# A decoder layer's routing: scratch in PSUM, one-hots eight tokens at a time, and two weight splits on another engine

## The chip, the cores and the metric

The kernel runs on one core of a Trainium2 chip. Its time is the device time of one execution in microseconds; of several runs the median counts. A core has TensorE (matrix products, into PSUM), VectorE, ScalarE and GpSimd, which work side by side, each through its own instructions in order, and queues that issue DMA transfers (SP's above all). VectorE and ScalarE reach both SBUF and PSUM; in this kernel GpSimd's operands are all in SBUF. PSUM has eight banks of 512 float32 values per partition.

## The reference

Two layers of a decoder work on 512 tokens of 1024 features. A layer has a token mixer, cross-attention into 256 memory rows, and a retrieval over 128 x 128 experts, each followed by a layer norm of the scaled input plus the result. The change lies in the second norm and in the first part of the retrieval:

```python
def peer_ffn(x, wq, k1, k2, u, v):
    qry = (x @ wq).reshape(B, S, PEER_HEADS, PEER_QDIM)            # 8 heads of 256
    s1 = jnp.einsum('bshc,nc->bshn', qry[..., :PEER_HALF], k1)     # 128 keys
    s2 = jnp.einsum('bshc,nc->bshn', qry[..., PEER_HALF:], k2)
    v1, i1 = lax.top_k(s1, PEER_TOPK)                              # 16
    v2, i2 = lax.top_k(s2, PEER_TOPK)
    cand = (v1[..., :, None] + v2[..., None, :]).reshape(B, S, PEER_HEADS, 256)
    sc, ci = lax.top_k(cand, PEER_TOPK)
    e1 = jnp.take_along_axis(i1, ci // PEER_TOPK, axis=-1)
    e2 = jnp.take_along_axis(i2, ci % PEER_TOPK, axis=-1)
    expert = e1 * N_KEYS + e2
    gate = jax.nn.softmax(sc, axis=-1)
    ...
        act = jax.nn.gelu(jnp.einsum('td,ted->te', xb, u[eb]), approximate=False)
        coef = (gb * act).astype(x.dtype)
        return jnp.einsum('te,ted->td', coef, v[eb])
```

## The kernel before

**Split products.** Large products are made in three passes: an operand is split into a high part (a cast on ScalarE, L224) and a low part (source minus high part, a subtraction, L225), and L229 to L231 multiply high by high, high by low and low by high. The subtraction runs on VectorE, or on GpSimd where the caller says so. `Weights` holds 256 columns of a projection as two pieces of 128 x 1024; `wahead(nl, ns)` issues the loads (L163, on SP's queue) and the splits of the groups that come next, on the engine in `weng`. `weights(ahead)` calls it and hands out the next group.

**Order.** The program is a list of instructions that a scheduler puts into an order for each engine, mostly that of the list; an instruction that is ready may pass one that is not. `weave` interleaves two streams of work by their estimated costs. SBUF scratch is handed out by `Arena`, in pages of 128 floats; memory that was given back first is given out first, so an instruction can wait for the last reader of what lay there before. PSUM tiles all come from one pool of eight banks (`bank`).

**Second norm.** `out_proj_ln` makes the rows of four blocks of 128 tokens; each block gets its residual (L312), statistics (L313, L319) and norm (L323, L300 to L304, L326) on VectorE, and is transposed (L280) and split for the queries. After it `body` sets `weng` to GpSimd and calls `queries`.

**Queries and routing.** `proj(h)` multiplies head h's query columns (48 instructions of 512 columns), copies the queries out (L791, ScalarE), makes the scores (L799) and copies them (L800). `main` does this for heads 1 to 7, with two chunks of the experts' first layer after each (one after heads 6 and 7); a chunk (`u_chunk`) is 24 products of 384 columns, with a Gelu on ScalarE (L1187), and its weights are split on GpSimd. Woven into it, `route(h)` runs on VectorE alone: for both halves of the keys `top16` finds the 16 largest values and their positions for each of four blocks (L840 to L848), L872 packs positions into bytes, L876 to L879 make 80 candidate sums, `top16` runs on these, and L885 to L906 decode the positions: which byte of which word belongs to each (L885 to L892), a shift count for four words (L898), the shift itself (L901), the maximum over the words (L903), a shift down (L905) and the expert's number (L906). All its scratch is in SBUF (`plain`).

**Gates.** Four chunks follow, then `gate_rows` for three blocks of 128 tokens, woven with two chunks, then four more chunks. Per block it splits the expert numbers into their two keys (L919 to L922), transposes them (L925) and the gates (L929), and for every four tokens makes a one-hot of the first key (L941, VectorE), multiplies it by the gates (L942, GpSimd), makes a one-hot of the second key (L948 on VectorE, or L945 and L946 on ScalarE for two of eight groups), multiplies the two (L951, TensorE) and copies the result (L952, ScalarE). The one-hots lie in the middle of SBUF, seven pieces of eight pages, of which the block's scratch `w` takes one. From 32 tokens on, a result goes to memory (L955) and comes back four chunks at a time in the dense part, where TensorE multiplies with all 128 chunks.

Of the kernel before, what the change touches and what calls it, by code (L numbers as in the profile page):

```python
# [65 lines left out]
def weave(*streams):  # L66
    """interleave generators that yield their costs, each with its estimated total"""
    live = [[g, 0.0, t] for g, t in streams]
    while live:
        s = min(live, key=lambda s: s[1] / s[2])  # L70
        try:
            s[1] += next(s[0])
        except StopIteration:
            live.remove(s)


class Arena:
# [21 lines left out]
    def take(self, shape, where):  # L99
        """where: 0 the first piece only, 2 its end, 1 the other pieces if possible, None any"""  # L100
# [37 lines left out]
class Split:  # L138
    """feature-major activations [128, 8, n] as two float32r parts, four blocks to a piece"""
# [13 lines left out]
class Weights:  # L153
    """256 (or fewer) columns of a projection: [128, 8, cols], loaded, then split"""
# [26 lines left out]
class K:  # L181
# [13 lines left out]
    def middle(self, arena):  # L195
        """hands the middle of SBUF to one of the two arenas"""
# [57 lines left out]
    def fm_proj(self, w, blocks, xT, outs, halves=None):  # L254
        """out [features, tokens] = w[:, 128 i:128 i + 128]^T x for i of blocks, if asked for by halves of the tokens,
        the first or the second half first"""
# [13 lines left out]
    def t_split(self, src, xT, tb, blocks):  # L270
        """src(i): [128 t, 128 f], to feature block blocks[i], tokens of tb"""
# [16 lines left out]
    def row(self, name, l):  # L288
        """a parameter vector on all partitions"""
# [5 lines left out]
    def rstd(self, out, var, scale, eps, t, v):  # L295
        """out = (var * scale + eps) ** -0.5; t and v are for the steps between"""
# [12 lines left out]
    def residual(self, x, f, q, st):  # L309
        """one half of the rows of a block of tokens, and its statistics"""  # L310
# [4 lines left out]
    def layer_norm(self, y, st, g, b):  # L315
        """layer norm of the rows of one block of tokens, in place"""
# [11 lines left out]
    def out_proj_ln(self, l, yT, order, gname, bname, X):  # L328
        """X <- LN(ALPHA X + y @ w); returns the split transpose of the new rows"""
# [25 lines left out]
    def mixer(self, l, xT):  # L355
# [41 lines left out]
        def gates():  # L397
            """forget gates: cumulative log sigmoid on partitions 0..3"""
# [89 lines left out]
    def feat_rms(self, ys, gcol, yT, b0):  # L488
        """root mean square of 256 features on partitions, times the gain, to blocks b0, b0 + 1"""
# [94 lines left out]
    def stick(self, h, P, sp, ls, ys):  # L584
# [3 lines left out]
        for j in reversed(range(NT)):  # L588
# [3 lines left out]
            if j + 1 < NT:  # L592
                nc.tensor.matmul(tb[:, 128:n], self.ones, sp[j + 1], start=False, stop=True)
                if j:
                    # the sum of the blocks of keys from j on
                    nc.gpsimd.tensor_add(sp[j][:, 128:], sp[j][:, 128:], sp[j + 1])
# [13 lines left out]
    def rglru(self, xp, gate):  # L610
# [4 lines left out]
        # per feature: 8 softplus(-lam), and halves of the biases of the sigmoids  # L615
# [13 lines left out]
        for i in range(2):  # L629
# [5 lines left out]
            # u = x (1 + 0.044715 x^2) of the output gate's gelu  # L635
# [5 lines left out]
        for i in range(2):  # L641
# [3 lines left out]
            # sigmoid(z) = (1 + tanh(z / 2)) / 2  # L645
# [7 lines left out]
            # 1 - a^2 = tanh(w) (1 + a^2), a = exp(-w)  # L653
# [18 lines left out]
    def mem_kv(self, l, kv):  # L672
        """keys (feature-major) and values (rows) of the memory, by head"""
# [102 lines left out]
    def queries(self, l, xT, peer):  # L776
        """queries, scores and top experts of all tokens"""
# [5 lines left out]
        def proj(h):  # L783
            w = self.weights()
            q = []
            for b in ([0, 1],) if h == 0 else ([0], [1]):
                bks = [self.bank() for _ in b]
                emit(self.fm_proj(w, b, xT, bks, None if h else 0))
                for bk in bks:
                    q.append(self.al((S,)))  # L790
                    nc.scalar.copy(q[-1], bk)  # L791
            w.free()
# [10 lines left out]
        def main():  # L803
            """the rest of the queries, and chunks of the experts' first layer"""
# [19 lines left out]
    def softmax(self, v):  # L824
        """of the 16 scores of each head, the largest first: [t, head, 16]"""
# [10 lines left out]
    def top16(self, groups):  # L836
        """sorted 16 largest and their positions of each (values, largest, positions); spoils the values"""
# [12 lines left out]
    def route(self, h, sc, ga, ef):  # L850
        """top experts of one head for all tokens: their scores to ga, their numbers to ef"""
        nc = self.nc
        ta, tb, sh = self.al((896,)), self.al((NT, NC)), self.al((2 * NT, 4, TOPK))
        part = lambda o, *s: ta[:, o:o + int(np.prod(s))].rearrange(
            "p (t n) -> p t n" if len(s) == 2 else "p (t i n) -> p t i n", t=s[0],
            **({} if len(s) == 2 else dict(i=s[1])))
        v = part(0, NT, 2, TOPK)
        ix = part(128, NT, 2, TOPK).bitcast(U32)
        i8 = ta[:, 256:288].bitcast(U8)
        ti = part(288, NT, TOPK).bitcast(U32)  # L860
        tv = ga[:, :, h, :]
        q = part(416, NT, TOPK).bitcast(U32)
        m = part(480, NT, TOPK).bitcast(U32)
        d = part(544, NT, TOPK)
        r = part(608, NT, 2, TOPK)
        en = part(736, NT, 2, TOPK).bitcast(U32)
        for i in range(2):
            self.top16([(sc[:, t, i, :], v[:, t, i, :], ix[:, t, i, :]) for t in range(NT)])
            yield 4.3
        self.fr(sc)  # L870
        # the numbers as bytes, four to a word
        nc.vector.tensor_copy(i8, ta[:, 128:256].bitcast(U32))  # L872
        # candidates: (0, 0..15), (1..7, 0..7), (8..15, 0)
        v1, v2 = v[:, :, 0, :], v[:, :, 1, :]
# [8 lines left out]
        # position q + m, m < 8: (0, m) for q = 0, (0, 8 + m) for 8, (q / 8 - 1, m) for 16..64, (8 + m, 0) for 72;  # L883
        # all in units of an eighth
        nc.vector.tensor_scalar(q, ti, 120, None, op0=OP.bitwise_and)  # L885
        nc.vector.tensor_scalar(m, ti, 7, 3, op0=OP.bitwise_and, op1=OP.logical_shift_left)
        nc.vector.scalar_tensor_tensor(d, q, 72.0, m, op0=OP.is_equal, op1=OP.mult)
# [455 lines left out]
```

## Time and profile before

| what | value |
|---|---|
| median of 3 runs | 3571.64 us (3571.11 to 3574.22) |
| the profiled execution's span, first to last instruction | 3569.5 us |
| mean granted clock of TensorE | 0.984 |
| TensorE busy (products) | 3431.9 us, 96% |
| VectorE busy | 2599.8 us, 73% |
| ScalarE busy | 1433.2 us, 40% |
| GpSimd busy | 1149.4 us, 32% |
| HBM traffic | 206 GB/s over the span |

A row of the profile gives an engine's line in the kernel, the operation, what it writes and reads (`out<-in`, by the program's tiles: `plain`, `mid` and `parts` are SBUF, `bk` is a PSUM bank, `x` the activations), shapes, and a count. In a timeline the first numbers are start and duration, and the bracket is the engine's idle time before the instruction with what it waited for. Neighbouring instructions of one engine overlap by some 0.1 us. DVE is VectorE, ACT ScalarE, POOL GpSimd, PE TensorE and PEld its weight loads. PEclk is the share of TensorE's full clock that was granted.

### The profile page before, as it was taken

The page shows a single profiled execution, that of the slowest core. Times are in us where ns is not written, and L with a number is a line of the kernel's source. Part 1 is how long each engine was busy: PE and PEld are TensorE (multiplying, and loading weights), DVE is VectorE, ACT ScalarE, POOL GpSimd, SP SyncE. Part 2 cuts the span into 40 slices and gives each one's busy share as a digit, 9 for nine tenths or more (in the row PEclk, how much of TensorE's full clock was granted, in tenths as well). Part 3 has the DMA queues.
Part 4 walks back from the last instruction along what each step waited for, and adds up shares of the span by engine and source line. Part 5 has one row for each costly group of instructions (what it writes and reads, how often), then busy time and mean ns, then how long its engine had stood idle before and what let it go on. Part 6 is the DMA issues. An engine that isn't in the chain of part 4 may idle for free.

```text
span 3569.5 us, 50379 instructions
## 1 busy us (share of the span) xinstructions
PE 3431.9 (96%) x18546; PEld 3027.0 (85%) x18546; DVE 2599.8 (73%) x5122; ACT 1433.2 (40%) x2411; POOL 1149.4 (32%) x833
## 2 busy tenths in 40 slices
PE   9999989799999999999999999887999999999998
PEld 6678878788999999999876788777989999999987
DVE  4675489987777777777746754899777777777776
ACT  5653232573333333333345533325633333333332
POOL 0110043583334333433101000535733433334340
PEclk9999999999999999999999999998999999999999
DMA  4142221369888888888511322223698888888883
GB/s 169 59 131 71 85 83 61 118 247 334 303 302 292 295 303 294 294 300 284 200 51 59 124 77 79 83 66 130 258 332 300 298 300 288 308 295 294 296 293 117
DMA packets 278568, 738.17 MB, mean 207 GB/s; under 512 B 21424, under 2 KB 119984, under 8 KB 275248
## 3 DMA queue, kind: packets, MB, share of 16 engines
q1 hardware_dynamic: 204592, 466.47, 38.7%
q0 software_dynamic: 73728, 268.47, 20.3%
q8 instruction: 146, 2.39, 0.3%
q14 instruction: 102, 0.84, 0.1%
HBM read 682.43 MB, written 52.43 MB: 206 GB/s over the span
## 4 chain that ended last, share of the span: by engine, by line
PE 84%; DVE 13%; DMA 1%; ACT 1%; issue 1%; POOL 1%; DVEq 0%; SPq 0%; POOLq 0%; ACTq 0%
PE bk L229 24%; PE bk L231 24%; PE bk L230 24%; PE bk L951 5%; DVE plain L848 1%; DVE plain L844 1%; DVE plain L842 1%; PE bk L770 1%; DVE plain L840 1%; DVE plain L846 1%; PE bk L571 1%; PE bk L741 1%; DVE plain L901 1%; PE bk L527 1%; DVE x L326 1%
## 5 line engine op out<-in xcount | busy, mean ns | idle before, releaser
L231 PE MATMUL bk<-parts 128*128 128x512 f32 (+1 forms) x3746 | 1352.0, 361 | 0.3
L230 PE MATMUL bk<-parts 128*128 128x384 f32 (+2 forms) x3752 | 1334.9, 356 | 0.0
L229 PE MATMUL bk<-parts 128*128 128x384 f32 (+1 forms) x3554 | 1278.2, 360 | 2.3 <-ACT parts L224 2.3
L224 ACT CAST parts<-plain 128x1024 fp32r<-128x1024 f32 (+2 forms) x787 | 658.1, 866 | 1270.7 <-PE bk L230 1146.0
L225 DVE TENSOR_TENSOR parts<-plain,parts 128x384 fp32r<-128x384 f32 (+2 forms) x743 | 727.1, 983 | 513.5 <-ACT parts L224 484.9
L231 PEld LDWEIGHTS bk<-parts 128*128 128x128 f32 x3746 | 704.8, 188 | 68.8 <-issue 1.5
L230 PEld LDWEIGHTS bk<-parts 128*128 128x128 f32 x3752 | 707.3, 189 | 63.7
L229 PEld LDWEIGHTS bk<-parts 128*128 128x128 f32 x3554 | 669.8, 188 | 65.0 <-ACT parts L224 2.9
L976 POOL DMA_INDIRECT mid<-peer_u,plain x256 | 359.0, 1402 | 561.7 <-DVE plain L1011 430.4
L976 POOL DMA_INDIRECT mid<-peer_v,plain x256 | 364.5, 1424 | 544.5 <-DVE mid L999 443.6
L229 PE MATMUL bk<-parts,mid 128*128 128x512 f32 (+2 forms) x912 | 350.8, 387 | 11.3 <-ACT mid L224 7.9
L230 PE MATMUL bk<-parts,mid 128*128 128x512 f32 (+2 forms) x912 | 326.7, 359 | 5.1 <-DVE parts L225 5.1
L1011 DVE SCALAR_TENSOR_TENSOR plain<-mid,plain 128x1024 f32<-128x1024 f32 x256 | 327.7, 1280 | 1.5
L999 DVE SCALAR_TENSOR_TENSOR mid<-mid,x 128x1024 f32<-128x1024 f32 x256 | 309.2, 1219 | 0.0
L231 PE MATMUL bk<-parts,mid 128*128 128x512 f32 (+2 forms) x720 | 253.1, 353 | 0.0
L224 ACT CAST mid<-plain 128x1024 fp32r<-128x1024 f32 x163 | 168.7, 1037 | 201.3 <-PE bk L231 102.1
L229 PE MATMUL bk<-mid,parts 128*128 128x256 f32 (+1 forms) x798 | 237.0, 297 | 0.0
L231 PE MATMUL bk<-mid,parts 128*128 128x256 f32 (+1 forms) x798 | 229.0, 287 | 0.0
L229 PEld LDWEIGHTS bk<-parts,mid 128*128 128x128 f32 (+1 forms) x912 | 172.5, 190 | 57.2 <-issue 16.7
L951 PE MATMUL bk<-mid 128*128 128x128 f32 x1536 | 198.9, 292 | 17.1 <-POOL mid L942 16.4
L951 PEld LDWEIGHTS bk<-mid 128*128 128x128 f32 x1536 | 190.8, 198 | 25.0 <-POOL mid L942 21.5
L225 POOL TENSOR_TENSOR mid<-plain,mid 128x1024 fp32r<-128x1024 f32 x24 | 58.1, 2430 | 469.6 <-ACT mid L224 437.7
(229 smaller groups left out, 3940.9 us busy)
## 6 DMA issues: line engine op xcount, KB each, us to landing
plain<-peer_uT SPq DMA_DIRECT2D x256, 512.0 KB, 5.1
plain<-peer_v SPq DMA_DIRECT2D x256, 512.0 KB, 4.1
gates<-plain SPq DMA_DIRECT2D x24, 2048.0 KB, 6.9
plain<-gates SPq DMA_DIRECT2D x64, 768.0 KB, 8.0
plain<-w_in SPq DMA_DIRECT2D x44, 512.0 KB, 5.1
plain<-xa_wkv SPq DMA_DIRECT2D x32, 512.0 KB, 4.2
plain<-peer_wq SPq DMA_DIRECT2D x32, 512.0 KB, 4.1
plain<-w_out SPq DMA_DIRECT2D x16, 512.0 KB, 4.4
```

Of the source, the lines that this page charges most:

```text
L224: nc.scalar.copy(hi, src)
L225: return (eng or nc.vector).tensor_sub(lo, src, hi.bitcast(F32))
L229: nc.tensor.matmul(out, lt[0], rt[0], start=first, stop=False)
L230: nc.tensor.matmul(out, lt[0], rt[1], start=False, stop=False)
L231: nc.tensor.matmul(out, lt[1], rt[0], start=False, stop=last)
L326: nc.vector.scalar_tensor_tensor(y[:, h], y[:, h], rs, b[:, h], op0=OP.mult, op1=OP.add)
L527: nc.tensor.matmul(sb[:, :n], P["fq"][r][po, i * 128:n], P["fk"][r][po, :n], start=True, stop=True)
L571: nc.tensor.matmul(zb[:, :n], P["sk"][r][po, q0:q0 + 128], P["sq"][r][po, q0:], start=True, stop=True)
L951: nc.tensor.matmul(bk[:, k, :], o2[:, k, :], o1[:, k, :], start=True, stop=True)
L976: nc.gpsimd.indirect_dma_start(out=t, out_offset=None, in_=self.a[n], in_offset=bass.IndirectOffsetOnAxis(ap=ei[:, s:s + 1], axis=0))
L999: nc.vector.scalar_tensor_tensor(u, u, 1.0, x, op0=OP.mult, op1=OP.mult, accum_out=act[:, s:s + 1])
L1011: nc.vector.scalar_tensor_tensor(acc, v, act[:, s:s + 1], acc, op0=OP.mult, op1=OP.add)
```

## The change

The scratch of `route` moves to two PSUM banks, `ps` and `pi`, such that each decode instruction has at most one operand in SBUF; the shift down becomes two instructions. `gate_rows` keeps its integer steps in a bank, and works on eight tokens at a time; ScalarE makes the second one-hot of every third group of eight. The first two query weight groups are split on VectorE: `weng` is set to GpSimd inside `proj(0)`, after its products, and the second group's split is issued there too. Comments are also taken out, without effect.

```diff
 def proj(h):
-    w = self.weights()
+    w = self.weights() if h else self.weights(0)
...
             nc.scalar.copy(q[-1], bk)
+    if h == 0:
+        self.wahead(2, 1)
+        self.weng = nc.gpsimd
     w.free()
...
 def route(self, h, sc, ga, ef):
-    ta, tb, sh = self.al((896,)), self.al((NT, NC)), self.al((2 * NT, 4, TOPK))
+    ta, tb, sh = self.al((512,)), self.al((NT, NC)), self.al((2 * NT, 4, TOPK))
+    ps, pi = self.bank(), self.bank((128, 2 * NT, 4, TOPK))
...
-    v = part(0, NT, 2, TOPK)
-    ix = part(128, NT, 2, TOPK).bitcast(U32)
...
+    v1 = part(ps, 0, NT, TOPK)
+    ix = part(ps, 64, NT, 2, TOPK).bitcast(U32)
+    ti = part(ps, 192, NT, TOPK).bitcast(U32)
+    m = part(ps, 256, NT, TOPK).bitcast(U32)
+    r = part(ps, 320, NT, 2, TOPK)
+    e1 = part(ps, 448, NT, TOPK).bitcast(U32)
+    v2 = part(ta, 0, NT, TOPK)
+    i8 = ta[:, 64:96].bitcast(U8)
+    q = part(ta, 128, NT, TOPK).bitcast(U32)
+    d = part(ta, 192, NT, TOPK)
+    e2 = part(ta, 256, NT, TOPK).bitcast(U32)
...
-    si, su = sh.bitcast(I32), sh.bitcast(U32)
+    si, su = pi.bitcast(I32), sh.bitcast(U32)
...
-    nc.vector.tensor_tensor(su, words[:, :, :, None].to_broadcast(shape), su, op=OP.logical_shift_left)
+    nc.vector.tensor_tensor(su, words[:, :, :, None].to_broadcast(shape), pi.bitcast(U32),
+                            op=OP.logical_shift_left)
+    en = part(ps, 320, NT, 2, TOPK).bitcast(U32)
...
-    nc.vector.tensor_scalar(en, en, 24, None, op0=OP.logical_shift_right)
-    nc.vector.scalar_tensor_tensor(ef[:, :, h, :], en[:, :, 0, :], float(NK), en[:, :, 1, :],
-                                   op0=OP.mult, op1=OP.add)
+    nc.vector.tensor_scalar(e1, en[:, :, 0, :], 24, None, op0=OP.logical_shift_right)
+    nc.vector.tensor_scalar(e2, en[:, :, 1, :], 24, None, op0=OP.logical_shift_right)
+    nc.vector.scalar_tensor_tensor(ef[:, :, h, :], e1, float(NK), e2, op0=OP.mult, op1=OP.add)
...
 def gate_rows(self, tb, ga, ef, dram, stages):
+    pe = self.bank((128, 4, 128)).bitcast(I32)
...
-    sh = [128, 4, NK]
+    GB = 8
+    sh = [128, GB, NK]
...
-        for q in range(0, GT, 4):
+        for q in range(0, GT, GB):
...
-            if q % 12 == 8:
-                for k in range(4):
+            if t // GB % 3 == 2:
+                for k in range(GB):
...
-            bk = self.bank((128, 4, NK))
-            for k in range(4):
-                nc.tensor.matmul(bk[:, k, :], o2[:, k, :], o1[:, k, :], start=True, stop=True)
-            nc.scalar.copy(stage[:, :, q:q + 4], bk.rearrange("p t e -> p e t"))
+            for b in range(0, GB, 4):
+                bk = self.bank((128, 4, NK))
+                for k in range(4):
+                    nc.tensor.matmul(bk[:, k, :], o2[:, b + k, :], o1[:, b + k, :], start=True, stop=True)
+                nc.scalar.copy(stage[:, :, q + b:q + b + 4], bk.rearrange("p t e -> p e t"))
...
 def body(self, out):
...
-        self.weng = nc.gpsimd
         self.queries(l, xT, peer)
```

## Rows read from the trace of the kernel before

**Rows 1.** Busy time by stretch: start:end, length, engines (instructions), clock, DMA share, GB/s.
```profile
424.00:484.00 60.00, 49.56 (x380) 47.31 (x379) 47.55 (x64) 20.27 (x31) 20.97 (x9) 0.91 0.28 91
484.00:680.00 196.00, 171.15 (x887) 154.46 (x885) 181.33 (x924) 61.77 (x94) 70.22 (x31) 0.92 0.20 62
680.00:793.00 113.00, 102.86 (x785) 98.26 (x786) 101.24 (x167) 91.13 (x212) 100.68 (x100) 0.97 0.56 226
815.00:1770.00 955.00, 954.86 (x4777) 862.13 (x4778) 709.60 (x906) 344.13 (x488) 355.08 (x249) 1.00 0.84 293
```

**Rows 2.** TensorE's waits from 424 to 815 us: total, times, longest.
```profile
PE bk L925 <- DVE mid L922: 18.2, 1, 18.2
```

**Rows 3.** Timeline of VectorE in the second norm: start, duration, instruction.
```profile
427.22 1.23 DVE L225 TENSOR_TENSOR mid<-plain,mid 128x1024 fp32r<-128x1024 f32 x1 [1.15 <-ACT mid L224]
...
439.33 0.15 DVE L301 TENSOR_TENSOR ln_r<-ln_t 128x1 f32<-128x1 f32 x1
...
440.09 1.42 DVE L326 SCALAR_TENSOR_TENSOR x<-x,ln_r,plain 128x512 f32<-128x512 f32 x2
...
451.73 2.24 DVE L301 TENSOR_TENSOR ln_r<-ln_t 128x1 f32<-128x1 f32 x1
...
458.64 5.55 DVE L326 SCALAR_TENSOR_TENSOR x<-x,ln_r,plain 128x512 f32<-128x512 f32 x2
```

**Rows 4.** Timeline of GpSimd in the second norm.
```profile
451.16 5.13 POOL L225 TENSOR_TENSOR mid<-plain,mid 128x1024 fp32r<-128x1024 f32 x2 [191.69 <-ACT mid L224]
...
458.54 2.34 POOL L225 TENSOR_TENSOR mid<-plain,mid 128x1024 fp32r<-128x1024 f32 x1
```

**Rows 5.** Groups of VectorE's instructions, 484 to 672 us: busy us, mean ns, idle before.
```profile
L840 DVE MAX8 plain<-plain 128x8 f32<-128x128 f32 x64 | 14.8, 279 | 15.7 <-ACT plain L800 8.4 <-PE bk L799 7.2
L901 DVE TENSOR_TENSOR plain<-plain 128x512 uint32<-128x512 uint32 x8 | 13.9, 1736 | 0.2
...
L898 DVE TENSOR_TENSOR plain<-lanes,plain 128x512 int32<-128x512 f32 x8 | 9.5, 1193 | 0.3
...
L891 DVE TENSOR_TENSOR plain<-plain 128x64 f32<-128x64 uint32 x8 | 3.9, 492 | 0.2
```

**Rows 6.** Timeline of VectorE in the last head's route.
```profile
656.42 0.07 DVE L848 MATCH_VALUE_LOAD plain<-plain 128x8 f32 x1
...
663.49 0.23 DVE L891 TENSOR_TENSOR plain<-plain 128x64 f32<-128x64 uint32 x1
...
664.06 0.69 DVE L898 TENSOR_TENSOR plain<-lanes,plain 128x512 int32<-128x512 f32 x1
```

**Rows 7.** Timeline of TensorE in the routing.
```profile
484.88 0.49 PE L799 MATMUL bk<-plain 128*128 128x128 f32 x2
...
585.25 1.22 PE L799 MATMUL bk<-plain 128*128 128x128 f32 x4 [3.93 <-ACT plain L791]
...
632.68 0.39 PE L799 MATMUL bk<-plain 128*128 128x128 f32 x2
...
653.22 0.34 PE L231 MATMUL bk<-parts 128*128 128x384 f32 x1
```

**Rows 8.** Busy time of a stretch at half clock, columns as in rows 1.
```profile
583.30:596.90 13.60, 8.99 (x32) 8.48 (x33) 13.57 (x89) 4.23 (x6) 4.72 (x2) 0.50 0.24 78
```

**Rows 9.** Groups of instructions, 680 to 794 us, columns as in rows 5.
```profile
L951 PE MATMUL bk<-mid 128*128 128x128 f32 x752 | 97.4, 291 | 8.8 <-POOL mid L942 8.4
L942 POOL TENSOR_TENSOR mid<-mid,mid 128x512 f32<-128x512 f32 x94 | 94.6, 1040 | 9.5 <-DVE mid L941 8.7 <-DMA gates<-plain 0.2
...
L941 DVE TENSOR_TENSOR mid<-bk,iota 128x512 f32<-128x512 f32 x91 | 60.2, 682 | 5.5 <-ACT mid L930 4.5 <-PE bk L951 0.9
...
L946 ACT ACTIVATE mid<-mid 128x512 f32<-128x512 f32 x22 | 13.9, 631 | 0.5
```

**Rows 10.** Timeline of ScalarE in the gates.
```profile
674.10 1.57 ACT L945 ACTIVATE mid<-iota,mid 128x128 f32<-128x128 f32 x5
...
727.10 2.03 ACT L952 COPY plain<-bk 128x512 f32<-128x512 f32 x4
```

More of the change, by code (lines that the diff above doesn't have):

```diff
@@ L852, in route, with part @@
         nc = self.nc
-        ta, tb, sh = self.al((896,)), self.al((NT, NC)), self.al((2 * NT, 4, TOPK))
-        part = lambda o, *s: ta[:, o:o + int(np.prod(s))].rearrange(
-            "p (t n) -> p t n" if len(s) == 2 else "p (t i n) -> p t i n", t=s[0],
-            **({} if len(s) == 2 else dict(i=s[1])))
-        v = part(0, NT, 2, TOPK)
-        ix = part(128, NT, 2, TOPK).bitcast(U32)
-        i8 = ta[:, 256:288].bitcast(U8)
-        ti = part(288, NT, TOPK).bitcast(U32)
-        tv = ga[:, :, h, :]
[L862 to L868, printed above, removed]
+        ta, tb, sh = self.al((512,)), self.al((NT, NC)), self.al((2 * NT, 4, TOPK))
+        ps, pi = self.bank(), self.bank((128, 2 * NT, 4, TOPK))
+        def part(t, o, *s):
+            return t[:, o:o + int(np.prod(s))].rearrange(
+                "p (t n) -> p t n" if len(s) == 2 else "p (t i n) -> p t i n", t=s[0],
+                **({} if len(s) == 2 else dict(i=s[1])))
+        v1 = part(ps, 0, NT, TOPK)
[9 more added lines that the diff above has]
+        e2 = part(ta, 256, NT, TOPK).bitcast(U32)
+        tv = ga[:, :, h, :]
+        for i, v in enumerate((v1, v2)):
+            self.top16([(sc[:, t, i, :], v[:, t, :], ix[:, t, i, :]) for t in range(NT)])
             yield 4.3
         self.fr(sc)
-        nc.vector.tensor_copy(i8, ta[:, 128:256].bitcast(U32))
-        v1, v2 = v[:, :, 0, :], v[:, :, 1, :]
+        nc.vector.tensor_copy(i8, ps[:, 64:192].bitcast(U32))
         s1 = [128, NT, 7, 8]
@@ L886, in route @@
         nc.vector.tensor_scalar(m, ti, 7, 3, op0=OP.bitwise_and, op1=OP.logical_shift_left)
+        nc.vector.tensor_scalar(r[:, :, 0, :], q, 8.0, 0.0, op0=OP.subtract, op1=OP.max)
+        nc.vector.tensor_scalar(r[:, :, 1, :], q, 8.0, 64.0, op0=OP.is_equal, op1=OP.mult)
         nc.vector.scalar_tensor_tensor(d, q, 72.0, m, op0=OP.is_equal, op1=OP.mult)
-        nc.vector.tensor_scalar(r[:, :, 0, :], q, 8.0, 0.0, op0=OP.subtract, op1=OP.max)
         nc.vector.tensor_add(r[:, :, 0, :], r[:, :, 0, :], d)
-        nc.vector.tensor_scalar(r[:, :, 1, :], q, 8.0, 64.0, op0=OP.is_equal, op1=OP.mult)
         nc.vector.tensor_sub(d, m, d)
@@ L914, in gate_rows @@
         w = self.al((1024,), F32, 1)
-        ei = w[:, 896:1024].bitcast(I32)
-        i12 = w[:, 0:256].rearrange("p (a b) -> p a b", a=2).bitcast(I32)
         f12 = w[:, 256:512].rearrange("p (a b) -> p a b", a=2)
         st = w[:, 512:896].rearrange("p (a b) -> p a b", a=3)
-        nc.vector.tensor_copy(ei, ef[:, tb].rearrange("p h k -> p (h k)"))
-        nc.vector.tensor_scalar(i12[:, 0], ei, 7, None, op0=OP.logical_shift_right)
-        nc.vector.tensor_scalar(i12[:, 1], ei, 127, None, op0=OP.bitwise_and)
-        nc.vector.tensor_copy(f12, i12)
+        pe = self.bank((128, 4, 128)).bitcast(I32)
+        nc.vector.tensor_copy(pe[:, 0], ef[:, tb].rearrange("p h k -> p (h k)"))
+        nc.vector.tensor_scalar(pe[:, 1], pe[:, 0], 7, None, op0=OP.logical_shift_right)
+        nc.vector.tensor_scalar(pe[:, 2], pe[:, 0], 127, None, op0=OP.bitwise_and)
+        nc.vector.tensor_copy(f12, pe[:, 1:3])
         pt = self.bank((128, 3, 128))
@@ L931, in gate_rows @@
         yield 2
-        sh = [128, 4, NK]
+        GB = 8
+        sh = [128, GB, NK]
         io = self.iota[:, None, :].to_broadcast(sh)
-        col = lambda i, t: (st if i == 2 else pt)[:, i, t:t + 4, None].to_broadcast(sh)
+        col = lambda i, t: (st if i == 2 else pt)[:, i, t:t + GB, None].to_broadcast(sh)
         for g in range(128 // GT):
             stage = stages[:, g % 2]
-            for q in range(0, GT, 4):
+            for q in range(0, GT, GB):
                 t = g * GT + q
-                o1, o2 = (self.al((4, NK), F32, 1) for _ in range(2))
+                o1, o2 = (self.al((GB, NK), F32, 1) for _ in range(2))
                 nc.vector.tensor_tensor(o1, col(0, t), io, op=OP.is_equal)
                 nc.gpsimd.tensor_mul(o1, o1, col(2, t))
-                if q % 12 == 8:
-                    for k in range(4):
+                if t // GB % 3 == 2:
+                    for k in range(GB):
                         nc.scalar.activation(o2[:, k], self.iota, AF.Abs, scale=-1.0, bias=st[:, 1, t + k:t + k + 1])
@@ L948, in gate_rows @@
                     nc.vector.tensor_tensor(o2, col(1, t), io, op=OP.is_equal)
-                bk = self.bank((128, 4, NK))
-                for k in range(4):
-                    nc.tensor.matmul(bk[:, k, :], o2[:, k, :], o1[:, k, :], start=True, stop=True)
-                nc.scalar.copy(stage[:, :, q:q + 4], bk.rearrange("p t e -> p e t"))
+                for b in range(0, GB, 4):
[3 more added lines that the diff above has]
+                    nc.scalar.copy(stage[:, :, q + b:q + b + 4], bk.rearrange("p t e -> p e t"))
                 self.fr(o1, o2)
-                yield 1.3
+                yield 2.6
             nc.sync.dma_start(dram[:, tb * (128 // GT) + g], stage)
```

## The prediction

> **What bounds the kernel now.** I read the busy time by stretch first [rows 1]. [...] The time to be had lies between 424 and 793 us, and in the same stretches of the second layer, which look alike. There TensorE is idle for 10.4 us in the second norm (424 to 484), 24.9 us in the routing (484 to 680) and 10.1 us in the gates (680 to 793), and the mean clock is 0.91, 0.92 and 0.97.
>
> The waits of TensorE say who is late: its longest is 18.2 us at the end of the routing, for VectorE's L922 [rows 2]. So the routing ends with VectorE (busy 181.3 of 196 us [rows 1]); the gates run on TensorE (102.9 of 113 us) with GpSimd (100.7) and VectorE (101.2) close behind.
>
> Then the instructions. In the second norm a clean second half of the layer norm (two of L326) takes 1.42 us; while GpSimd splits weights, L301 takes 2.24 instead of 0.15 us and the two of L326 take 5.55 us [rows 3]; GpSimd's splits stand in exactly these microseconds [rows 4]. In the routing L901 has a mean of 1.74 us, L898 1.19, L891 0.49 [rows 5], where an undisturbed one takes 0.69 (L898; L901 has the same 512 elements) and 0.23 us [rows 6]. MAX8, which also reads SBUF, has its clean 0.28 us in all 64 cases [rows 5]. What is stretched is the decode steps, by a GpSimd split that runs at that moment.
>
> **The change, part by part; one layer.**
>
> *Norm.* The splits of the first two query weight groups (four subtractions of 128x1024) go from GpSimd to VectorE. VectorE loses the stretching: in the third block of tokens 2.1, 2.1, 1.9 and 4.1 us for L301, L302, L304 and L326, in the fourth 2.1, 1.7 and 1.5, together 15.5 us (the first and the last of the third block are shown [rows 3]). It gains 4 x 1.23 = 4.9 us [rows 3]. One GpSimd split stays, the experts' first, which preload gives to GpSimd by name, and so perhaps 2 us of stretching. ScalarE's casts stay the same in number. The second group's split, and the load of the third group on SP's queue, are issued after head 0's products: both are needed a head later, and ScalarE and SP idle there. A new wait: head 0's first product waits for VectorE's split, which stands behind the third block's norm; behind it TensorE holds that block's transposes. Net VectorE -8 to -10 us. TensorE's idle 10.4 us and about 3 us of low clock bound the gain at 13; if the new wait costs what a norm of a block costs (some 6 us from residual to transposes, of which half is hidden), 6 are left. I take **-10 us** (6 to 13).
>
> *Routing.* After the change every decode step has at most one operand in SBUF. The stretching summed over eleven decode groups (mean less clean, times 8: 8.5 for L901, 4.0 for L898, and 1.3 to 2.2 for each of the other nine, as L891's 8 x 0.26 = 2.1) is 30 us [rows 5, 6]. Without it VectorE has 181.3 - 30 = 151 us of work in the stretch, of which about 10 are softmax and one-hots: 18 us for each of 8 heads. One more instruction per head (the two shifts) costs 0.1. But TensorE then feeds VectorE: from 484.88 to 653.56 us it works 168.7 us [rows 7], of which 6.6 are two gaps near 585 (one of 3.93 is shown; ScalarE's copy waited there for memory that a late decode step held), and in the stretch at half clock that follows, 9.0 us busy were worth 4.5 [rows 8]. That is 157.6 us without both. The last head's scores come at 633 now [rows 7], hence at 622 then; a copy of 1 us, 18 us of route, 4 us of softmax and of the gates' first steps, and 1.5 us of the head before not yet done: 646.5 against 671.7 now, 25 us less. The 18.2 us wait shrinks to about 4.
>
> What PSUM costs VectorE is only half shown. L941 with an operand in PSUM takes 0.68 us for 512 elements [rows 9], L898 with both in SBUF 0.69 [rows 6]: no difference. No row has a MAX8, an index or an integer step that reads or writes PSUM. Above I bound it by one MATCH_VALUE_LOAD (0.07 us, [rows 6]) for each of the 27 instructions of a head that read PSUM: 1.9 us a head. As heads come every 21 us and a route takes 18, that shows only in the last two heads: 0 to 4 us. I take 1, near the row. Routing: **-24 us**; ends -27 (nothing for PSUM, no head late) and -17 (the gaps near 585 stay). [...]
>
> *Gates.* Per four tokens TensorE needs 8 of 752 instructions that fill 97.4 us, 1.04 us, and GpSimd one product, 94.6 us for 94, 1.01 us [rows 9]: level. With eight tokens the elements stay, and instructions halve on VectorE and GpSimd. I expect nothing back, since TensorE needs its 1.04 anyway. What is lost: (a) a block's first unit goes through VectorE and GpSimd before TensorE may start, 0.68 + 1.04 us now, about 1.25 + 2.0 then: +1.5 us at each of two boundaries between blocks, +3. (b) The two one-hots of a unit now fill two pieces of eight pages; six of the middle's seven pieces are left beside the block's scratch, so three units are in flight instead of six half as big. ScalarE builds five of 16 units a block: 8 x 0.31 for L945 (five in 1.57 us) and about 0.95 for a L946 twice as wide as one of 0.63, 3.4 us, and has 4 copies of 0.51 (four in 2.03 us) beside [rows 9, 10], all in the 4 us that TensorE needs for the two units before: 5.4 against 4.0, so up to 1.4 us lost at four units of three blocks, 17 us; nothing, if the copies give way. I take +2: four copies in one piece show that copies do give way to L945 now. (c) GpSimd's 1024-element product: twice 1.01, or the 2.34 us of a split, a product's width with another operation [rows 4]: 48 x 0.32 = 15 us more. I take twice 1.01; L942 is the same operation on the same kinds of operands. Gates: **+5 us** (0 to 20). The integer steps in a PSUM bank instead of SBUF save 1 to 3 us of VectorE off the path: nothing.
>
> Sum: -10 - 24 + 5 = -29 us a layer, -58 in all. The profiled execution's span of 3569.5 becomes 3511.5; the median of the runs is 2.1 us above that span, so 3571.6 becomes **3514 us**.
>
> **The rivals.**
> - *The units of eight starve TensorE through ScalarE*: (b) at its full 17. For it: ScalarE is at 91.1 of 113 us already [rows 1] and gets 25% more one-hots. Against: copies can wait, with banks free. -10 - 24 + 20 = -14 a layer: 3544.
> - *GpSimd's wide product costs what a split costs*, GpSimd becomes the bound of the gates: -10 - 24 + 18 = -16: 3540. Against: twice L942 is below it.
> - *All goes well*: no loss in the gates, 12 in the norm, 27 in the routing: -39, 3494.
> - *The change doesn't free the decode*: L872 and other steps with a single SBUF operand are held too, and each new step still has one. Then 3 us in the routing, 6 in the norm, 5 lost: 3564. Against: MAX8 has one SBUF operand and is never held, nor is L941 (0.68 in all cases, beside a GpSimd busy for 100.7 of 113 us).
> - *Slower: banks.* A route now holds two of eight PSUM banks for all its 18 us; a head's products, scores and two chunks ask for six. If banks are given out so that one request must wait for a route to end, TensorE can't run ahead: a head then takes 11 (products) + 2 + 1 + 18 = 32 us instead of 21, last scores at 709, the routing's end 59 us later: +54 a layer, about 3680. It decides from the seventh request within one route on.
>
> **How the numbers follow.** Forecast 0.44 (3500 to 3530), ScalarE's units 0.17, GpSimd's product 0.13, all well 0.15, decode not freed 0.05, banks 0.06. The range goes from the good case with its last bounds to just beyond the two gates cases: 3485 to 3556. This kernel's measurement tells about 0.2% (7 us) from no change. Faster: the first four, 0.89; same: 0.05; slower: 0.06.
>
> **What would show it.** Right: L901 and L898 near 0.69 us in all 16 cases; L301, L302 at 0.15 in the second norm; TensorE's wait for L922 under 6 us; no half clock in the routing. Wrong: L951 waiting for ScalarE's L946 or for a L942 of more than 2.0 us; TensorE's products waiting for a bank that VectorE's route releases; MAX8 or FIND_INDEX8 above 0.35 us. A half clock in the gates would add to any of the losses.

## The result, and the profile after

The changed kernel is slower. Its median is 3597.72 us (3591.16 to 3598.77) against 3571.38 for the kernel before: a ratio of 1.0068, 95% interval 1.0053 to 1.0082. The forecast was 3514 with a range to 3556. The profiled execution's span is 3589.5 us, 20.0 above that of before.

Both layers lost alike (9.4 and 10.5 us). The table cuts the first layer of several kernels at four events of TensorE's and VectorE's timelines: the first product with the keys (head 0's scores), the first transpose of the gates (L925 before, L935 after), the end of the last matmul of the gates (L951, L963), and the end of the layer's last residual. The other kernels are the experiments below.

| us | scores start | routing, to the transposes | gates | rest of the layer | layer ends |
|---|---|---|---|---|---|
| before | 483.2 | 188.5 | 121.0 | 992.0 | 1784.7 |
| after | 479.6 | 193.3 | 127.0 | 994.2 | 1794.1 |
| route_only | 485.3 | 195.2 | 121.1 | 991.0 | 1792.6 |
| gates_only | 483.0 | 188.9 | 128.7 | 994.3 | 1794.9 |
| norm_only | 478.3 | 188.4 | 120.6 | 991.7 | 1779.0 |
| wide_scratch | 478.6 | 192.5 | 130.1 | 992.6 | 1793.8 |
| top16_in_sbuf | 484.9 | 178.4 | 128.8 | 993.2 | 1785.3 |
| two_banks | 480.4 | 177.7 | 129.3 | 993.5 | 1780.9 |
| norm_and_decode | 479.5 | 179.9 | 122.6 | 994.1 | 1776.1 |
| norm_chunks_too | 474.9 | 187.6 | 120.8 | 992.0 | 1775.3 |
| three_units | 483.4 | 187.7 | 131.9 | 992.8 | 1795.8 |
| six_units | 482.0 | 186.8 | 123.0 | 996.7 | 1788.5 |
| norm_u_decode | 473.0 | 179.8 | 122.3 | 991.6 | 1766.7 |

The first column is the least sure: top16_in_sbuf, two_banks and after share one norm and lie 5 us apart. These 5 us stand ahead of the norm. From the norm's first residual (L312) to the first scores, all kernels with the old norm take 69.3 or 69.4 us, all with the norm of the change 65.8 or 65.9 (norm_chunks_too 60.9, norm_u_decode 59.4), in the second layer of before and after too (69.3 and 65.8). So of after's 9.4 us, the norm gave some 3.5 back, the routing took 4.8, the gates 6.0 and the rest of the layer 2.2.

Busy time of after by stretch, columns as in rows 1, whose stretches these answer to:

```profile
424.00:480.00 56.00, 48.77 (x378) 46.75 (x376) 43.66 (x68) 19.88 (x31) 12.07 (x5) 0.91 0.31 97
480.00:680.00 200.00, 168.41 (x885) 151.81 (x885) 175.02 (x927) 61.45 (x92) 69.45 (x30) 0.94 0.20 64
680.00:800.00 120.00, 98.34 (x791) 95.27 (x790) 91.82 (x85) 98.58 (x229) 94.90 (x52) 0.96 0.51 207
```

VectorE's 181.3 us in the routing [rows 1] were to become some 151; they are 175.0. In the gates every engine is now idle for over 20 of 120 us: a chain of waits bounds them, not one engine's work. TensorE's waits in after, 424 to 830 us (total, times, longest):

```profile
PE bk L935 <- DVE mid L932: 22.6, 1, 22.6
PE bk L963 <- POOL mid L953: 10.9, 4, 3.7
PE bk L963 <- ACT mid L957: 9.3, 11, 1.1
PE bk L280 <- DVE x L326: 6.2, 3, 4.1
```

The first answers to rows 2: 22.6 us where 18.2 stood and 4 was forecast. The next two are the gates' matmuls waiting for GpSimd's products and for ScalarE's one-hots. The aim of the change itself was reached. VectorE's groups of after, 480 to 680 us (busy us, mean ns, idle before):

```profile
L907 DVE TENSOR_TENSOR bk<-lanes,bk 128x512 int32<-128x512 f32 x8 | 5.6, 695 | 0.4
L910 DVE TENSOR_TENSOR plain<-plain,bk 128x512 uint32<-128x512 uint32 x8 | 5.4, 680 | 0.1
...
L901 DVE TENSOR_TENSOR bk<-bk,plain 128x64 f32<-128x64 f32 x8 | 1.9, 232 | 0.3
...
L900 DVE TENSOR_TENSOR plain<-bk,plain 128x64 f32<-128x64 uint32 x8 | 1.8, 224 | 0.3
```

L910 and L907 are the L901 and L898 of rows 5, which had means of 1736 and 1193 ns; they now have their clean length while GpSimd splits as much as ever (69 of 200 us). So the question is what ate the gain.

### The profile page after: what moved, and what is told of

It reads as the page before. It is cut to its first block, busy times and chain, and to the rows that moved or that the text cites. A ratio compares the mean times of both kernels' runs of the same rounds, so it can differ in the third digit from the quotient of the medians.

```text
span 3589.5 us, 49948 instructions
## 1 busy us (share of the span) xinstructions
PE 3421.7 (95%) x18546; PEld 3017.5 (84%) x18546; DVE 2559.0 (71%) x4972; ACT 1446.9 (40%) x2441; POOL 1118.4 (31%) x729
## 5 line engine op out<-in xcount | busy, mean ns | idle before, releaser
L225 POOL TENSOR_TENSOR parts<-plain,parts 128x1024 fp32r<-128x1024 f32 x44 | 109.5, 2497 | 579.5 <-ACT parts L224 542.1
L963 PE MATMUL bk<-mid,mid 128*128 128x128 f32 x1536 | 188.7, 285 | 40.0 <-POOL mid L953 21.6
L963 PEld LDWEIGHTS bk<-mid,mid 128*128 128x128 f32 x1536 | 183.3, 199 | 45.3 <-POOL mid L953 27.8
```

The source lines that it names most:

```text
L225: return (eng or nc.vector).tensor_sub(lo, src, hi.bitcast(F32))
L963: nc.tensor.matmul(bk[:, k, :], o2[:, b + k, :], o1[:, b + k, :], start=True, stop=True)
```

## The experiments

**One part at a time.** Three kernels, each the kernel before with one function of the change. Ratios here and below are against runs of the kernel before that stand beside each group (medians 3572.9 to 3575.9 us).

```diff
 route_only: before, with the changed route()
 gates_only: before, with the changed gate_rows()
 norm_only: before, with
-    w = self.weights()
+    w = self.weights() if h else self.weights(0)
...
+    if h == 0: self.wahead(2, 1); self.weng = nc.gpsimd
...
-    self.weng = nc.gpsimd
```

> The kernel before with the change's routing alone (scratch in PSUM); norm and gates as before. Theory: two things cancel the freed decode. The decode steps lose their 33 us of held time a layer, the instructions of top16 that write a PSUM bank wait for each other and gain 24 us, and the first MAX8 waits for head 1's scores because the smaller scratch lies where head 1's query was: it starts about 10 us later, at 496 instead of 486.5 us. TensorE's wait for the gates' first step stays near 18 to 24 us; the time is 3565 to 3580 us. Rival, that the routing is the gain that was forecast and only the gates lose: first MAX8 near 487, that wait under 6 us, 3520 to 3535 us.

> The kernel before with the change's gates alone (eight tokens at a time, integer steps in a bank). Theory: ScalarE's share of the one-hots, every third unit, is late by 0.8 to 1.1 us at each of some 12 units a layer, and a block's first unit takes 1.4 us longer: +6 to +8 us a layer, 3583 to 3588 us. Rival, that the gates lose only in the company of the other parts: within 3 us of the kernel before, 3568 to 3575.

> The kernel before with the change's norm alone (the first two weight groups split on VectorE). Theory: GpSimd still does the experts' first split and the third group's in the norm and still holds up two steps of the last blocks; the first scores come 2 to 4 us earlier, 3563 to 3568 us. Rival, the full removal as forecast: first scores 10 us earlier, 3548 to 3555.

route_only: 3586.43 us, 1.0033 (1.0024 to 1.0043). gates_only: 3596.75 us, 1.0066 (1.0044 to 1.0089). norm_only: 3565.68 us, 0.9975 (0.9962 to 0.9989). The norm helps a little, as expected; the routing's scratch in PSUM, which the forecast counted on, is a loss by itself, 6 us above the upper end of its expectation; the gates are the largest loss, 9 us above theirs.

**The routing: a late start, or dearer sorting?** VectorE's timeline shows two new things in after. The routing starts late (the first MAX8 before, then in after):

```profile
486.52 0.49 DVE L840 MAX8 plain<-plain 128x8 f32<-128x128 f32 x2 [8.36 <-ACT plain L800]
```

```profile
492.93 0.29 DVE L843 MAX8 plain<-plain 128x8 f32<-128x128 f32 x1 [18.34 <-PE bk L802]
```

Scores begin 3.6 us earlier than before and MAX8 6.4 us later. It writes the second list's values into the 512-float scratch, which lies where head 1's query lay, and so it waits until head 1's scores (L802) have read that. And the index searches stand further apart. VectorE in the kernel before, then in after, near 520 us (start, duration, instruction):

```profile
520.61 0.29 DVE L842 FIND_INDEX8 plain<-plain 128x8 uint32<-128x128 f32 x1
520.81 0.07 DVE L842 MATCH_VALUE_LOAD plain<-plain 128x8 f32 x1
520.87 0.29 DVE L842 FIND_INDEX8 plain<-plain 128x8 uint32<-128x128 f32 x1
521.07 0.07 DVE L842 MATCH_VALUE_LOAD plain<-plain 128x8 f32 x1
521.12 0.29 DVE L842 FIND_INDEX8 plain<-plain 128x8 uint32<-128x128 f32 x1
```

```profile
520.10 0.29 DVE L851 FIND_INDEX8 bk<-bk,plain 128x8 uint32<-128x128 f32 x1
520.43 0.10 DVE L851 MATCH_VALUE_LOAD bk<-bk,plain 128x8 f32 x1
520.51 0.29 DVE L851 FIND_INDEX8 bk<-bk,plain 128x8 uint32<-128x128 f32 x1
520.84 0.10 DVE L851 MATCH_VALUE_LOAD bk<-bk,plain 128x8 f32 x1
520.92 0.29 DVE L851 FIND_INDEX8 bk<-bk,plain 128x8 uint32<-128x128 f32 x1
```

The durations are equal (0.29). But before, the next instruction starts 0.20 us after a search has started, while that one still runs, and the next search 0.26 us after the last; in after these are 0.33 and 0.41 us, and the search is over before anything starts. A sum of durations can't show that; the starts do. From start to start, less the waits for scores, the instructions of `top16` take 105 us a layer before and 128 in after (129 in wide_scratch, below); the rest of `route`, mostly the decode, takes 69.4 before and 44.1 after.

Two kernels part the causes. wide_scratch takes the late start away, top16_in_sbuf the writes of `top16` into PSUM as well.

```diff
 wide_scratch: after, with
-    ta, tb, sh = self.al((512,)), ...
+    ta, tb, sh = self.al((896,)), ...
 top16_in_sbuf: wide_scratch, with
-    v1 = part(ps, 0, NT, TOPK)
-    ix = part(ps, 64, NT, 2, TOPK).bitcast(U32)
-    ti = part(ps, 192, NT, TOPK).bitcast(U32)
+    v1 = part(ta, 0, NT, TOPK)
+    ix = part(ta, 128, NT, 2, TOPK).bitcast(U32)
+    ti = part(ta, 256, NT, TOPK).bitcast(U32)
...
```

> The changed kernel with the routing's SBUF scratch at its old size of 896 floats (more than it uses), which moves it off the memory of head 1's query. Theory: the first MAX8 no longer waits for head 1's scores and starts near 483 instead of 492.9 us, the routing's end comes 6 to 10 us a layer earlier, 3578 to 3586 us. Rival, that the late start comes from the PSUM banks: no change, 3595 to 3599.

> The run with the wide scratch, and in it all that top16 writes (both lists, their positions, the positions of the candidates) in SBUF; the decode's scratch stays in PSUM. Theory: top16 costs its old 105 us a layer instead of 129, while L882 to L894 read SBUF alone again and get some 8 us of held time back: VectorE's routing takes about 15 us less a layer, the wait for the gates' first step falls from 21.1 to 5 to 12 us, 3570 to 3580 us against 3594.6. Rival, that MAX8 and FIND_INDEX8 are slower for another reason than where they write: their sums stay, 3590 to 3597.

wide_scratch: 3594.58 us, 1.0051 (1.0035 to 1.0067). MAX8 starts at 481.9, 11 us earlier, and the routing is only 0.8 us shorter: VectorE now waits 8.8 us for head 1's scores instead, which come no earlier. The late start was real and almost free; the 6 to 10 us a layer that were expected did not come. top16_in_sbuf: 3564.25 us, 0.9974 (0.9964 to 0.9984), some 30 us below wide_scratch: `top16` is back at 105 us, and TensorE's wait at the end of the routing is 8.9 us (21.1 in wide_scratch). It did better than both its expectations.

**Is the write to PSUM dear, or the neighbour's write to the same bank?** In after all searches of a route write into one bank, but not all are followed at once by another such write. VectorE in after shows both kinds:

```profile
521.74 0.29 DVE L845 FIND_INDEX8 bk<-plain 128x8 uint32<-128x128 f32 x1
522.07 0.09 DVE L845 MATCH_VALUE_LOAD bk<-plain 128x8 f32 x1
522.14 0.29 DVE L845 FIND_INDEX8 bk<-plain 128x8 uint32<-128x128 f32 x1
522.35 0.07 DVE L847 MATCH_VALUE_LOAD plain<-plain 128x8 f32 x1
```

Of the 128 searches of this size in the first layer, 76 are followed by another one into the same bank, and there the next instruction starts 0.327 us later in the mean; 34 are followed by a step that neither reads nor writes PSUM, and there it starts after 0.202 us. two_banks puts the positions back into PSUM, but so that neighbours go to different banks:

```diff
 two_banks: top16_in_sbuf, with (even blocks of tokens in ps, odd ones in pi)
-    ix = part(ta, 128, NT, 2, TOPK).bitcast(U32)
-    ti = part(ta, 256, NT, TOPK).bitcast(U32)
+    ix = [part(t, 0, NT // 2, 2, TOPK).bitcast(U32) for t in (ps, pi.rearrange("p a b c -> p (a b c)"))]
+    ti = [part(t, 64, NT // 2, TOPK).bitcast(U32) for t in (ps, pi.rearrange("p a b c -> p (a b c)"))]
...
```

> The kernel of top16_in_sbuf (3564.25 us; sorted values and positions of top16 in SBUF, decode in PSUM, norm and gates of the changed kernel) with the positions alone put back into PSUM, but in two banks in turn, even blocks of 128 tokens in one, odd blocks in the other. So no position is written into a bank that the write just before it went to. Theory (an instruction that writes into a bank waits for the last write into that bank, and the write itself costs nothing): FIND_INDEX8 starts 0.19 to 0.22 us after the instruction before it, as with positions in SBUF (0.20), and the time is 3562 to 3572. Rival (writing positions to PSUM is itself dear): 0.30 to 0.34 us, as in the changed kernel (0.33), about 12 us more a layer: 3580 to 3592.

(What is left out makes the cast of the positions and the first two steps of the decode in halves, one for each bank.) It took 3566.89 us, 0.9982 (0.9972 to 0.9991), as its theory expected. VectorE's timeline in two_banks:

```profile
522.15 0.29 DVE L845 FIND_INDEX8 bk<-plain 128x8 uint32<-128x128 f32 x1
522.35 0.07 DVE L845 MATCH_VALUE_LOAD bk<-plain 128x8 f32 x1
522.41 0.29 DVE L845 FIND_INDEX8 bk<-plain 128x8 uint32<-128x128 f32 x1
522.61 0.07 DVE L845 MATCH_VALUE_LOAD bk<-plain 128x8 f32 x1
522.67 0.30 DVE L845 FIND_INDEX8 bk<-plain 128x8 uint32<-128x128 f32 x1
```

The same instruction, still writing to PSUM, is followed after 0.20 us again (a mean of 0.202 over the 128 cases of this size on either line). So a write to PSUM is not dear in itself; the price, 0.13 us each time, is paid where neighbours go to the same bank, and the second starts only after the first has ended. Whether the bank makes it wait or a wait that is written into the program, no run here tells apart. Shown for FIND_INDEX8; for MAX8, which has the same lengthening in after (L849 into the bank, 0.34 for 0.19 us), it is inferred by likeness.

**The gates: how many units, or how big?** three_units keeps the four-token one-hots of before, but takes the double memory for each, so that three small units are in flight. six_units keeps the eight-token units of gates_only and finds memory for six.

```diff
 three_units: before, with
-    o1, o2 = (self.al((4, NK), F32, 1) for _ in range(2))
+    p1, p2 = (self.al((8, NK), F32, 1) for _ in range(2))
+    o1, o2 = p1[:, :4], p2[:, :4]
...
 six_units: gates_only, with
-    o1, o2 = (self.al((GB, NK), F32, 1) for _ in range(2))
+    o1, p2 = self.al((GB, NK), F32, 1), self.al((GB, NK), F32R)
+    o2 = p2.bitcast(F32)
...
```

> The kernel before with its four-token one-hots in tiles of twice the size, half unused, so that three units are in flight instead of six; instructions are the same. If it is the number of units in flight that starves TensorE: 12 to 25 us a layer, 3595 to 3620 us. If it is the size of ScalarE's piece of work, whatever is in flight: within 8 us, 3568 to 3580.

> The kernel of gates_only (3596.75 us; the kernel before with the one-hots eight tokens at a time) with the second one-hot of a unit in the memory for parts of products, so that six units of eight tokens are in flight instead of three. Theory (the number of units in flight starves TensorE): the matmuls' waits for ScalarE's and GpSimd's one-hots (8.6 and 11.4 us) fall below 3 us each, the last of the gates' matmuls ends at 791 to 795 us, as before (792.7; 800.6 with three), and the time is 3568 to 3580. Rival (the pieces of eight tokens are too big for ScalarE or GpSimd): the waits stay, the gates end at 798 to 801 and the time is 3588 to 3598.

three_units: 3602.21 us, 1.0087 (1.007 to 1.0104). Fewer units in flight cost the old gates 10.9 us a layer (121.0 to 131.9), with no instruction made bigger. six_units: 3582.58 us, 1.0025 (1.0012 to 1.0039). Depth gives 5.7 of gates_only's 7.7 us back (128.7 to 123.0), and the waits for ScalarE, 8.6 us in gates_only, are gone. The time is still 2.6 us above the upper end of what was expected, for two reasons. GpSimd's wait went up, not down (TensorE's waits of six_units, 424 to 830 us):

```profile
PE bk L953 <- POOL mid L943: 14.8, 6, 3.7
```

(11.4 in gates_only, 8.4 before [rows 9]), and the rest of the layer is 4.7 us longer than before. Most of that is one place some 20 us behind the gates, where TensorE waits 4.0 us for ScalarE's cast of weights (1.5 before), which stands behind VectorE's first step on gates that come back from memory; 3.4 us at half clock follow there (none before), an estimated 1.7 us lost. What TensorE waits for on GpSimd is seen in the latter's timeline in six_units:

```profile
780.54 2.38 POOL L225 TENSOR_TENSOR parts<-plain,parts 128x1024 fp32r<-128x1024 f32 x1
782.87 1.90 POOL L943 TENSOR_TENSOR mid<-mid,mid 128x1024 f32<-128x1024 f32 x1
784.91 0.98 POOL L978 DMA_INDIRECT mid<-peer_u,plain  x1
785.91 3.75 POOL L943 TENSOR_TENSOR mid<-mid,mid 128x1024 f32<-128x1024 f32 x2
```

Products of 1.9 us stand in one queue with splits and gathers, and here TensorE waited for three of them.

**The norm: whose splits?** In after, GpSimd still splits in the second norm. GpSimd's timeline in after:

```profile
453.43 9.06 POOL L225 TENSOR_TENSOR parts<-plain,parts 128x1024 fp32r<-128x1024 f32 x3 [194.00 <-ACT parts L224]
466.10 2.37 POOL L225 TENSOR_TENSOR parts<-plain,parts 128x1024 fp32r<-128x1024 f32 x1 [3.61 <-ACT parts L224]
```

These four are the experts' chunks (`parts`, where rows 4 have `mid`, the queries' weights). The same four stand in the norm before, between the queries' splits and behind them (GpSimd before; rows 4 leave them out):

```profile
456.25 2.34 POOL L225 TENSOR_TENSOR parts<-plain,parts 128x1024 fp32r<-128x1024 f32 x1
...
460.84 2.79 POOL L225 TENSOR_TENSOR parts<-plain,parts 128x1024 fp32r<-128x1024 f32 x1
...
469.84 4.74 POOL L225 TENSOR_TENSOR parts<-plain,parts 128x1024 fp32r<-128x1024 f32 x2
```

With the queries' splits gone they come earlier, and VectorE is held by them (VectorE in after):

```profile
454.84 1.55 DVE L304 TENSOR_TENSOR ln_r<-ln_r,ln_t 128x1 f32<-128x1 f32 x1
457.45 5.58 DVE L326 SCALAR_TENSOR_TENSOR x<-x,ln_r,plain 128x512 f32<-128x512 f32 x2
466.27 2.22 DVE L301 TENSOR_TENSOR ln_r<-ln_t 128x1 f32<-128x1 f32 x1
```

norm_chunks_too gives the first four chunks to VectorE; norm_and_decode and norm_u_decode add to norm_only and to norm_chunks_too the route of top16_in_sbuf, with the gates as before.

```diff
 norm_chunks_too: norm_only, with
-    self.split(self.uq, 0, self.k.nc.gpsimd)
+    self.split(self.uq, 0)
...
-    self.split(self.uq, c + 1, k.nc.gpsimd if c + 1 < AHEAD else None)
+    self.split(self.uq, c + 1, k.nc.gpsimd if 4 <= c + 1 < AHEAD else None)
```

> The run with the norm alone, and in it the experts' first four chunks split on VectorE too. In the norm's trace GpSimd still did four splits there, all of expert chunks. Theory: they are what still holds L304, L326 and L301 (1.53, 5.58, 2.24 us); without them these take 0.15, 1.42 and 0.15, VectorE gets 4 x 1.2 us of splits, and the first scores come 2 to 6 us earlier: 3554 to 3562 us. Rival, that VectorE's own added work stands in the way: no change or later, 3564 to 3572.

> The kernel before with the change's norm, and the routing of the last run (decode in PSUM, top16 in SBUF, wide scratch); gates by four tokens as before. If the parts add: norm 8 us and routing 10 to 15 us a layer below the kernel before, 3536 to 3552 us. Rival, that VectorE's saved time is lost again because TensorE and ScalarE pace the routing: the norm's gain alone, 3562 to 3568.

> The kernel of norm_and_decode (3550.92 us: queries' splits on VectorE during the second norm, decode in PSUM with top16 in SBUF, gates as before) with the first four chunks of the experts' weights split by VectorE too, so that GpSimd splits nothing during the second norm. Theory (the norm is held by the splits that GpSimd finds time for, whoever's they are, and the two gains add): L301 and L304 near 0.15 and 0.23 us in all blocks of the second norm, and a further 10 to 14 us gone, as from norm_only (3565.68) to norm_chunks_too (3554.73): 3536 to 3544. Rival (VectorE, which now ends the routing, has to do the four splits of 1.2 us in the routing, and they cost there what they gain in the norm): 3547 to 3553.

norm_chunks_too: 3554.73 us, 0.9948 (0.9931 to 0.9965). norm_and_decode: 3550.92 us, 0.9937 (0.992 to 0.9954). norm_u_decode: 3538.09 us, 0.9889 (0.987 to 0.9907), faster than both kernels of this study. In norm_chunks_too, VectorE's groups in the norm, 424 to 478 us, have no held instruction left:

```profile
L326 DVE SCALAR_TENSOR_TENSOR x<-x,ln_r,plain 128x512 f32<-128x512 f32 x8 | 5.6, 747 | 0.1
...
L301 DVE TENSOR_TENSOR ln_r<-ln_t 128x1 f32<-128x1 f32 x4 | 0.6, 150 | 0.0
```

In norm_only the same groups have means of 1268 and 672 ns. All three times lie inside what was expected, and the gains add up. norm_chunks_too is 18.2 us below the runs of before beside it, the decode brings 13.6 (norm_and_decode is 22.0 below its, norm_only 8.4 below its), together 31.8; norm_u_decode is 37.8 below (33 to 46 by its interval).

## Why the prediction was wrong, step by step

- **What bounds the kernel, and what stretches the decode:** right. L907 and L910 are clean in all 16 cases, and 25 us of VectorE's time a layer are gone (69.4 to 44.1), for which the sum of rows 5 less rows 6 said 30. That a single operand in SBUF is harmless was too wide: L975, a step from SBUF to SBUF with one operand, took 1.59 us beside GpSimd's splits in after (shown under the tail, below) and 0.22 before, and L885 of before, with one operand too, up to 2.34. The decode steps of after that stayed clean beside splits read or write PSUM.
- **Routing -24 (-27 to -17): it was +4.8, and this step decides the sign.** The term that failed is the price of PSUM, "1" us with a bound of 1.9 a head. It was worked out from what an instruction costs that reads PSUM. The cost came from order: instructions that had overlapped their neighbours' ends now start behind them, +23 us a layer, 3 a head, in every head, and VectorE became the limit again. The timeline of before would have allowed a better bound: MAX8 takes 0.28 us [rows 5], but its neighbour starts 0.20 after it, so each of hundreds of instructions overlaps the next, and a wait takes at least that overlap (0.09 of FIND_INDEX8's 0.29 us, where 0.13 was paid). The sum of durations, on which the forecast of 151 us rests, leaves such overlaps out. That heads come every 21 us, so that the price shows in two heads only, fell with it.
- **TensorE feeding VectorE, last scores at 622:** failed too, by about 10 us, even where `top16` is cheap. From the first to the last scores TensorE takes 149.6 us before, 148.4 in top16_in_sbuf and 148.0 in norm_u_decode (145.6 in two_banks, 144.6 in after, where the half clock of rows 8 is gone: the mean clock of this stretch is 0.99 and 1.00 there, 0.95 before); the forecast needed some 138. Nor did the half clock go: 20.9 us of the routing run at it in after, 27.0 before. The gaps of 6.6 us near 585 [rows 7] were put down to late decode steps. They stay with the decode freed (TensorE in norm_u_decode, then ScalarE there):

```profile
578.48 2.93 PE L802 MATMUL bk<-plain 128*128 128x128 f32 x12 [4.83 <-ACT plain L791]
```

```profile
571.68 0.59 ACT L791 COPY plain<-bk 128x512 f32<-128x512 f32 x1 [8.06 <-DVE bk L914]
572.16 1.05 ACT L224 CAST mid<-plain 128x1024 fp32r<-128x1024 f32 x1
576.89 1.04 ACT L224 CAST mid<-plain 128x1024 fp32r<-128x1024 f32 x1 [3.67 <-DMA plain<-peer_wq]
577.84 0.58 ACT L791 COPY plain<-bk 128x512 f32<-128x512 f32 x1
```

  ScalarE's copy waits for memory that a route gives back at its end (8.06 us; 12.86 before), then a cast waits for a load of weights (3.67; 3.33 before), and the next copy stands behind it. The route is shorter and the gap is not. So with `top16` cheap again the routing gains 8.6 to 10.8 us, not 24: in top16_in_sbuf what comes after the last scores shrinks from 38.9 to 30.0 us, and little else. In after this part grew to 48.7 us: there the loss stands.
- **The tail:** not in the sum. In after GpSimd's splits fall on the softmax's last step, which still has two operands in SBUF: 2.05 us where the same step took 0.68 before (L834 there). With its neighbour these are 2.7 us; the last head's L901 had lost 2.1 in their place (2.78 us before, at 664.79 us). In the last head the stretching was moved and not removed (VectorE in after; GpSimd splits from 666.20 to 673.61 us):

```profile
667.05 2.05 DVE L837 TENSOR_TENSOR plain<-plain,gsum 128x512 f32<-128x512 f32 x1
...
669.79 1.59 DVE L975 TENSOR_SCALAR plain<-plain 128x128 int32<-128x128 f32 x1
```

- **Norm -10 (6 to 13): it was some -3.5 in either layer.** The step "One GpSimd split stays" failed: four stayed, the experts' chunks. They stood in the timeline of before, between the lines of rows 4, and could have been counted there; without the queries' splits GpSimd makes them earlier. The held L301, L302, L304 and L326 lose 7.9 of 15.6 us (their groups of 424 to 484 us sum to 23.0 before, to 15.1 in after, to 7.4 in norm_chunks_too), and VectorE's own four splits cost 4.9. With these chunks moved too the norm is 8.4 us shorter (60.9 for 69.3 from its first residual), near the 10. The feared new wait for head 0's products doesn't appear.
- **Gates +5 (0 to 20): +6.0, inside, but by two errors that nearly cancel.** (a) A block's first unit: TensorE waits 3.65 us (gates_only, two boundaries) where it waited 2.27, so +2.8 for the two, as sized. (b) The three units in flight: 9.3 us of waits for ScalarE where +2 was taken; the mechanism of the first rival, at half its price. (c) The wide product is cheaper than twice the narrow one. GpSimd in after, 680 to 800 us, beside L942 in rows 9:

```profile
L953 POOL TENSOR_TENSOR mid<-mid,mid 128x1024 f32<-128x1024 f32 x47 | 88.4, 1897 | 23.1 <-DVE mid L952 23.1
```

  1897 for 2 x 1040 ns: the rival of a wide product at a split's 2.34 us is out. "I expect nothing back" erred the other way. For the same 826 instructions of the gates TensorE is busy 105.3 us in after (105.3 to 108.6 in all kernels with eight-token units) and 110.8 before, so 5.4 us came back, and its longer waits (10.9 and 9.3 us for products and one-hots, 8.4 and none before) were paid from that in part.
- **The rest of the layer, +2.2, was not foreseen.** The old gates don't keep it away: norm_and_decode has them, and 994.1. Half of it is seen: the wait behind the gates for ScalarE's cast is 2.6 us in after and 1.5 before (4.0 in six_units, 2.3 in norm_and_decode). Why it grows, and what the other half is, stays open.
- **The rivals:** the banks came true as a word only. TensorE waited for a bank of a route once in the first layer (3.1 us for L910, at 641 us, after the last scores, where it has time to spare); what cost was inside one engine, between its writes to one bank. No rival named that; the 0.06 for slower stood for another mechanism.
- **What an instruction that reads PSUM costs:** L882, a cast from PSUM, takes 292 ns in after and 218 with its source in SBUF (norm_u_decode), 74 more. The decode's small steps show 0 to 40 ns: L901 with a PSUM operand takes 232 ns, and its clean forerunner in SBUF 0.23 us [rows 6]. Even 74 ns for each of the 27 instructions of a head that read PSUM would be an estimated 2.0 us a head, near the bound of 1.9, and 16 us in all eight heads of a layer: less than the 24 of the forecast, so that this alone would not have turned the sign.

## What to carry to other kernels

Before moving the results of a run of short instructions into one PSUM bank, read from the timeline how far each overlaps the next. Where the starts lie closer than the durations (here 0.20 us for 0.29), try neighbours in different banks (two_banks kept the 0.20), or in SBUF; in one bank it was 0.33, and `top16` took 128 us a layer for 105. When buffers get bigger, count how many fit: three units in flight instead of six cost 10.9 us a layer here, with the same instructions (three_units). And when an engine is to be kept quiet in a stretch, look at what else it will find to do there (in after four splits, beside which two of L326 took 5.58 us for 1.42).

## What was not expected of the hardware

- Behind a FIND_INDEX8 of 128x128 whose neighbour writes to the same PSUM bank, the next VectorE instruction starts 0.33 us later (after); with neighbours in two banks in turn (two_banks), or in SBUF (before), 0.20 us, at the same duration of 0.29 us.
- GpSimd's product of 128x1024 takes 1.90 us (L953 in after), two of 128x512 take 2.08 (2 x 1040 ns, L942 in rows 9).
